# Inverses from 16x16 blocks made row by row on VectorE, and half of the mixers' low parts on GpSimd

## The chip, the cores and the metric
The kernel runs on one core of one Trainium2 chip. The metric is the device time of one execution in microseconds (us); the profile adds, for one such execution, every instruction of the five engines with its start and duration: TensorE (PE, with its weight loads shown apart as PEld), VectorE (DVE), ScalarE (ACT), GpSimd (POOL) and SyncE (SP), which issues the DMAs.

## The reference
A decoder trunk of two layers over 256 tokens of width 2048, all in float32. Each layer is a token mixer followed by a SwiGLU block, both between an adaptive scale and shift (from a conditioning vector `c`) and a layer norm. Layer 0 mixes with mLSTM heads and RWKV-7 heads, layer 1 with retention heads and gated DeltaNet (gdn) heads. Cut to what the change touches:

```python
def _gated_deltanet(q, k, v, z, a, b, conv_w, a_log, dt_bias, norm_g):
    ...
    ut = jnp.eye(CHUNK, dtype=f32) + jnp.where(strict, jnp.einsum('cbhtd,cbhsd->cbhts', kb, kc) * gamma, 0.0)
    u = lax.linalg.triangular_solve(ut, vc * bc[..., None], left_side=True, lower=True)
    ...

def _rwkv7(z, mu, w0, w2, a0, a2, g2, k_k, k_a, r_k, ln_g, ln_b):
    ...
    def step(S, inp):
        rt, wt, kt, vt, at, bt = inp
        sa = jnp.einsum('bhij,bhj->bhi', S, at)
        S = S * wt[:, :, None, :] + sa[..., None] * bt[:, :, None, :] + vt[..., None] * kt[:, :, None, :]
        return S, jnp.einsum('bhij,bhj->bhi', S, rt)
    ...

def _mixer_cd(h, positions, w_in, w_out, ret_norm_g, conv_w, a_log, dt_bias, gdn_norm_g):
    proj = h @ w_in
    ...
    return jnp.concatenate([yc, yd], -1) @ w_out
```
Both recurrences are turned into chunked matrix form (chunks of 128 tokens in the kernel), and each chunk and head needs the inverse of a 128x128 unit triangular matrix. The large products (`h @ w_in` and the like) are dense.

## The kernel before
**Products.** A product of the 256 tokens with 512 columns of weights runs over "units". A unit (`unit`, lines 342 to 359) loads 1 MB of weights into a buffer `raw` (three buffers, shared with the conditioning work), and `split` (lines 326 to 340) turns it into two halves, each as a high part `hi`, rounded by ScalarE (L337), and a low part `lo = raw - hi`, by VectorE (L338). `hi` and `lo` have three buffers each, of one half. For each half, two token tiles and two row blocks, PE does three matmuls: activations high by weights high (L357), high by low (L358), low by high (L359), so 12 matmuls per half and 24 per unit.

**Conditioning.** `ada_unit` (L289) multiplies a 1 MB row block of `ada_w` with `silu(c)` on VectorE and sums it, 192 times in the kernel. `fill` places them behind units at a rate: 48 behind the 44 units of the first mixer, 48 behind the 68 units of the second.

**Inverses.** `rwkv_heads` runs four times (batches of four heads by two chunks) and `gdn_group` twice; each makes eight 128x128 matrices on PE (scores: L776, L1106), writes them to `mk[:, 0]` or `ma[:, 0]`, masks them on GpSimd (`keep_upper` L642, `unit_diagonal` L646) and calls `inverses`. That one starts from inverses of 2x2 blocks (transposes L611, masks L612 on VectorE and L613 on GpSimd) and doubles the block six times, from 2 to 64. A level is: a matmul of the matrix with the blocks so far (L622), a mask (L626, VectorE), a matmul with the transposed blocks (L629), an addition (L632, VectorE), eight transposes (L636) and their copy to `dt` by ScalarE (L637). The results go on to L798 (rwkv) and L1136 (gdn).

**GpSimd** besides: decays of mLSTM (L952, masked at L642) and gdn (L1099), and the sums of the rotary embedding (L1212, L1213).

**Order.** A planner fixes the order on each engine at build time by priorities: program order, with `split` moved ahead by 2000 instructions (`high_priority(offset=2000)`). At run time each engine works through its list in order and waits on semaphores.

**Order of the program:** `first_products` (16 units, before the mixers), `mixer_ab` (rwkv, then mLSTM), `mix_out`, a SwiGLU block, `mixer_cd` (gdn group 0, gdn group 1, retention), `mix_out`, the second SwiGLU block.

Of the kernel before, what the change touches and what calls it, by code (L numbers as in the profile page):

```python
# [13 lines left out]
AF = mybir.ActivationFunctionType  # L14
ALU = mybir.AluOpType
# [4 lines left out]
P = 128  # L20
# [9 lines left out]
LN_EPS = 1e-5  # L30
DH = 128
DECAY = -math.exp(-0.5)
LEVELS = (2, 4, 8, 16, 32, 64)


COLS = {}
# [7 lines left out]

CONS = {}
_n = 0
for _name, _w in [("ident", 128), ("cum", 256), ("tr", 128), ("ones", 128), ("sl", 128), ("m2", 128), ("m2t", 128),
                  ("lev", 64 * len(LEVELS)), ("bones", 128), ("hsel", 2), ("freq", 64)]:
    CONS[_name] = (_n, _w)
    _n += _w  # L50
# [3 lines left out]
def constants():  # L54
    i = np.arange(P)
    c = np.zeros((P, NCONS), np.float32)

    def put(name, a):
        o, w = CONS[name]
        c[:, o:o + w] = a  # L60

    u, t = i[:, None], i[None, :]
    put("ident", np.eye(P))
    after = ((u > 63) & (u <= t)).astype(np.float64) - ((u <= 63) & (u > t))
    before = ((u > 63) & (u < t)).astype(np.float64) - ((u <= 63) & (u >= t))
# [4 lines left out]
    put("m2", (u // 2 == t // 2) & (t <= u))  # L70
    put("m2t", (u // 2 == t // 2) & (u <= t))
# [114 lines left out]
class Trunk:  # L186
    def __init__(self, tc, ins, out, stack):
        self.tc, self.nc, self.ins, self.out = tc, tc.nc, ins, out

        def pool(name, bufs, **kw):  # L190
            return stack.enter_context(tc.tile_pool(name=name, bufs=bufs, **kw))

        self.fix = pool("fix", 1)
        self.raw_p = pool("raw", 3)
        self.split_p = pool("split", 3)
        self.h_p = pool("hp", 4)
        self.a_p = pool("ap", 5)
        self.y_p = pool("yp", 3)
        self.mix = pool("mix", 1)
        self.ps_g = pool("psg", 4, space=PSUM)  # L200
        self.ps_m = pool("psm", 3, space=PSUM)
        self.ps_c = pool("psc", 1, space=PSUM)
        self.dram = pool("scratch", 1, space=DRAM)
        self.n = 0


    def name(self, s):
# [119 lines left out]
    def split(self, src, n, ahead=2000):  # L327

        nc = self.nc
        with self.tc.high_priority(offset=ahead):  # L330
            w = self.raw(src)
            parts = []
            for i in range(2):
                hi = self.split_p.tile([P, 1024], F32R, tag="hi", name=self.name("hi"))
                lo = self.split_p.tile([P, 1024], F32R, tag="lo", name=self.name("lo"))
                ws = w[:, 2 * n * i:2 * n * (i + 1)]
                nc.scalar.activation(hi[:, :2 * n], ws, AF.Copy)  # L337
                nc.vector.tensor_tensor(lo[:, :2 * n], ws, hi[:, :2 * n], ALU.subtract)  # L338
                parts.append((hi, lo))
        return parts  # L340

# [258 lines left out]
    def inverses(self, mt, dd):  # L600


        nc, v = self.nc, self.nc.vector
        d, dt = dd[:, 0], dd[:, 1]
        halves = [slice(0, 4), slice(4, 8)]
        m2, m2t = (self.con(n).unsqueeze(1).to_broadcast([P, 4, P]) for n in ("m2", "m2t"))
        four = lambda x: x.rearrange("p (h t) -> p h t", h=4)
        for hs in halves:
            b = self.bank()
            for j in range(4):  # L610
                nc.tensor.transpose(b[:, P * j:P * j + P], mt[:, hs.start + j, :], self.ident)  # L611
            v.tensor_tensor(d[:, hs, :], four(b[:]), m2, ALU.mult)  # L612
            nc.gpsimd.tensor_tensor(dt[:, hs, :], mt[:, hs, :], m2t, ALU.mult)  # L613
        lev = self.con("lev")
        for n, size in enumerate(LEVELS):
            dv = d.rearrange("p h (n two b) -> p h n two b", two=2, b=size)
            mask = lev[:, 64 * n:64 * n + 64].unsqueeze(1).to_broadcast([P, 4, 64])
            b, p = [], []
            for hs in halves:
                x = self.bank()  # L620
                for j in range(4):
                    nc.tensor.matmul(x[:, 64 * j:64 * j + 64], mt[:, hs.start + j, :], dv[:, hs.start + j, :, 0, :], start=True, stop=True)  # L622
                b.append(x)
            for x in b:
                p.append(self.own([P, 4, 64], "P", 2))
                v.tensor_tensor(p[-1][:], four(x[:, 0:256]), mask, ALU.mult)  # L626
            for hs, x, y in zip(halves, b, p):
                for j in range(4):
                    nc.tensor.matmul(x[:, 256 + 64 * j:320 + 64 * j], dt[:, hs.start + j, :], y[:, j, :], start=True, stop=True)  # L629
            for hs, x in zip(halves, b):  # L630
                o = dv[:, hs, :, 0, :]
                v.tensor_tensor(o, x[:, 256:512].rearrange("p (h n b) -> p h n b", h=4, b=size), o, ALU.add)  # L632
            for hs in halves:
                x = self.bank()
                for j in range(4):
                    nc.tensor.transpose(x[:, P * j:P * j + P], d[:, hs.start + j, :], self.ident)  # L636
                nc.scalar.activation(dt[:, hs, :], four(x[:]), AF.Copy)  # L637
# [7 lines left out]
    def unit_diagonal(self, x, n):  # L645
        self.nc.gpsimd.affine_select(x, x, pattern=[[0, n], [1, P]], compare_op=ALU.not_equal, fill=1.0, base=0, channel_multiplier=-1)  # L646


    def shifted(self, out, src, mu, rows=P):
# [113 lines left out]
    def rwkv_heads(self, B):  # L763
        nc, v = self.nc, self.nc.vector
        mm = nc.tensor.matmul
        ar, bk, rho = B["ar"], B["bk"], B["rho"]
        mk = self.a8([P, 2, 8, P])
        rbkr = self.a8([P, 8, 2, P])
        heads = [(c, h) for c in range(2) for h in range(2)]
        for t in range(NT):  # L770
            for c, h in heads:
                r = slice(64 * h, 64 * h + 64)
                j = 4 * t + 2 * c + h
                b = self.bank()
                for x in range(2):
                    mm(b[:, T * x:T * x + T], bk[r, c, x, t, :], ar[r, c, t].rearrange("p x s -> p (x s)"), start=True, stop=True)  # L776
                nc.scalar.activation(mk[:, 0, j, :], b[:, 0:P], AF.Copy, scale=rho[:, t, 2 * c + h:2 * c + h + 1])
                nc.scalar.activation(mk[:, 1, j, :], b[:, 2 * P:3 * P], AF.Copy)
                v.tensor_copy(rbkr[:, j], b[:].rearrange("p (k x s) -> p k x s", k=2, x=2)[:, :, 1, :])
            js = slice(4 * t, 4 * t + 4)  # L780
            self.keep_upper(mk[:, :, js, :], [2, 4], True)
            self.unit_diagonal(mk[:, 0, js, :], 4)
            self.keep_upper(rbkr[:, js], [4, 2], False)
        dt = self.inverses(mk[:, 0], self.y8([P, 2, 8, P]))
        V = B["vb"][:, 0]
# [2 lines left out]
        for t in range(NT):  # L788
            xb = self.bank()
            for c, h in heads:  # L790
                d = 2 * c + h
# [3 lines left out]
            x = self.t1([P, T])  # L795
# [5 lines left out]
            for c, h in heads:  # L801
                d = 2 * c + h
# [31 lines left out]
        b = self.bank()  # L834
# [216 lines left out]
    def gdn_group(self, g, product, rest, gates=None):  # L1051
# [43 lines left out]
        for t in range(NT):  # L1095
# [166 lines left out]

    def mixer_ab(self, h, rate, early):
        self.yT = {}
        self.rwkv(h, rate, early)
        self.mlstm_gates()
        for g in range(2):
            self.mlstm_group(g, self.ins["w_ab"], h, rate)

    def mixer_cd(self, h, rate):  # L1270
        self.yT = {}
        w = self.ins["w_cd"]
        at = [0]

# [23 lines left out]
            self.retention_group(g, product)  # L1298

    def mix_out(self, w, x, sub):  # L1300
        y = [self.y8([P, D]) for _ in range(NT)]
        self.gate = self.gate_rows()
        stats = [self.tiny([P, 24], "st", 2) for _ in range(NT)]
# [46 lines left out]
```

## Time and profile before

| what | us |
|---|---|
| median of three runs | 2915.05 (2909.9 to 2915.27) |
| the profiled execution | 2917.53 |
| its span, first to last instruction | 2914.8 |
| four rwkv inverses and what lies between them | about 222 to 550 |
| dense products of mLSTM | about 600 to 690 |
| first and second gdn inverse | 1690 to 1740, 1820 to 1890 |
| retention | about 1890 to 2060 |

The page of a profile gives busy time per engine, then groups of equal instructions: line, engine, operation, the tile written and the tiles read, shape, count; then busy time, mean duration in ns, and the idle time of the engine just before them with what ended it. A timeline row is: start, duration, engine, line, operation, tiles, shape, count. A row of the windows is: the stretch, its length, then the busy time of each engine in it. PE's granted clock was 0.976 of full speed over the span. The matmuls' own durations overlap: a 512-column matmul shows 0.39 us and one starts every 0.23 us.

### The profile page before, as it was taken

The page shows a single profiled execution, that of the slowest core. Times are in us where ns is not written, and L with a number is a line of the kernel's source. Part 1 is how long each engine was busy: PE and PEld are TensorE (multiplying, and loading weights), DVE is VectorE, ACT ScalarE, POOL GpSimd, SP SyncE. Part 2 cuts the span into 40 slices and gives each one's busy share as a digit, 9 for nine tenths or more (in the row PEclk, how much of TensorE's full clock was granted, in tenths as well). Part 3 has the DMA queues.
Part 4 walks back from the last instruction along what each step waited for, and adds up shares of the span by engine and source line. Part 5 has one row for each costly group of instructions (what it writes and reads, how often), then busy time and mean ns, then how long its engine had stood idle before and what let it go on. Part 6 is the DMA issues. An engine that isn't in the chain of part 4 may idle for free.

```text
span 2914.8 us, 34843 instructions
## 1 busy us (share of the span) xinstructions
PE 2760.8 (95%) x13466; PEld 2291.6 (79%) x13466; DVE 2011.9 (69%) x2955; ACT 1276.3 (44%) x1685; POOL 123.5 (4%) x114
## 2 busy tenths in 40 slices
PE   3699999999999999999998999999989999999997
PEld 2578887877778888888887888877878888888886
DVE  7876666687777557767758878687786545556556
ACT  2264345446454444444445545343444444443442
POOL 0001111020000000000000121101000000000000
PEclk9799999999999999999999999999999999999998
DMA  9974234367578668867855756477656656667563
GB/s 366 356 277 170 91 134 159 131 242 267 199 249 305 249 219 296 297 236 275 305 197 205 295 209 241 159 277 295 216 202 231 249 195 224 242 220 241 192 216 130
DMA packets 106189, 674.62 MB, mean 231 GB/s; under 512 B 12068, under 2 KB 14248, under 8 KB 28328
## 3 DMA queue, kind: packets, MB, share of 16 engines
q1 hardware_dynamic: 106024, 672.41, 64.1%
q8 instruction: 105, 1.72, 0.2%
q14 instruction: 60, 0.49, 0.0%
HBM read 663.97 MB, written 8.39 MB: 231 GB/s over the span
## 4 chain that ended last, share of the span: by engine, by line
PE 62%; DVE 5%; DMA 3%; issue 1%; ACT 1%; POOL 1%; POOLq 0%; DVEq 0%; ACTq 0%
PE g L359 19%; PE g L358 19%; PE g L357 19%; DMA raw<-ada 2%; DVE lo L338 2%; DVE raw L289 1%; PE m L622 1%; PE m L629 1%; PE m L575 1%; ACT hi L337 1%; DMA raw<-gu 1%; DMA raw<-w_cd 0%; PE m L524 0%; PE c L317 0%; PE m L636 0%
## 5 line engine op out<-in xcount | busy, mean ns | idle before, releaser
L338 DVE TENSOR_TENSOR lo<-raw,hi 128x1024 fp32r<-128x1024 f32 (+2 forms) x848 | 1025.4, 1215 | 653.6 <-ACT hi L337 650.3
L337 ACT ACTIVATE hi<-raw 128x1024 fp32r<-128x1024 f32 (+2 forms) x848 | 885.7, 1049 | 1165.6 <-PE g L359 1004.1
L357 PE MATMUL g<-hi,h 128*128 128x512 f32 (+3 forms) x2368 | 932.7, 396 | 80.3 <-ACT hi L337 76.5
L358 PE MATMUL g<-lo,h 128*128 128x512 f32 (+3 forms) x2368 | 934.1, 395 | 3.8 <-DVE lo L338 3.8
L359 PE MATMUL g<-hi,h 128*128 128x512 f32 (+3 forms) x2368 | 930.9, 394 | 0.0
L357 PEld LDWEIGHTS g<-hi,h 128*128 128x128 f32 x2368 | 451.9, 191 | 172.0 <-ACT hi L337 78.8
L358 PEld LDWEIGHTS g<-lo,h 128*128 128x128 f32 x2368 | 452.6, 191 | 95.2 <-DVE lo L338 9.1
L359 PEld LDWEIGHTS g<-hi,h 128*128 128x128 f32 x2368 | 452.0, 191 | 88.6 <-issue 2.7
L289 DVE SCALAR_TENSOR_TENSOR raw<-raw,silu_c 128x2048 f32<-128x2048 f32 x176 | 404.4, 2298 | 23.1 <-DMA raw<-ada 22.8
L359 PE MATMUL g<-hi,a 128*128 128x512 f32 x960 | 374.5, 390 | 0.0
L357 PE MATMUL g<-hi,a 128*128 128x512 f32 x960 | 374.4, 390 | 0.0
L358 PE MATMUL g<-lo,a 128*128 128x512 f32 x960 | 374.1, 390 | 0.1
L358 PEld LDWEIGHTS g<-lo,a 128*128 128x128 f32 x960 | 180.3, 188 | 37.4 <-DVE lo L338 0.5
L359 PEld LDWEIGHTS g<-hi,a 128*128 128x128 f32 x960 | 180.3, 188 | 36.9
L357 PEld LDWEIGHTS g<-hi,a 128*128 128x128 f32 x960 | 180.2, 188 | 37.0
L1099 POOL TENSOR_SCALAR s<-cons_sb,log_alpha 128x128 f32<-128x128 f32 x16 | 22.9, 1446 | 1040.6 <-PE g L359 903.4
L637 ACT ACTIVATE y<-m 128x512 f32<-128x512 f32 x48 | 27.4, 595 | 78.3 <-PE m L636 78.1
L902 DVE SCALAR_TENSOR_TENSOR f<-c,cols_sb,f 128x255 f32<-128x255 f32 (+2 forms) x120 | 57.2, 477 | 6.2 <-ACT f L900 5.1
L626 DVE TENSOR_TENSOR P<-m,cons_sb 128x256 f32<-128x256 f32 x72 | 30.1, 423 | 43.6 <-PE m L622 43.2
L629 PEld LDWEIGHTS m<-P,y 128*128 128x128 f32 x384 | 50.0, 203 | 2.1 <-issue 0.3
L622 PEld LDWEIGHTS m<-y,a 128*128 128x128 f32 x384 | 49.7, 205 | 0.8
L622 PE MATMUL m<-y,a 128*128 128x64 f32 x384 | 49.7, 283 | 0.0
(376 smaller groups left out, 2051.2 us busy)
## 6 DMA issues: line engine op xcount, KB each, us to landing
raw<-ada SPq DMA_DIRECT2D x176, 1024.0 KB, 5.5
raw<-gu SPq DMA_DIRECT2D x176, 1024.0 KB, 4.8
raw<-dn SPq DMA_DIRECT2D x88, 1024.0 KB, 4.8
raw<-w_cd SPq DMA_DIRECT2D x60, 1024.0 KB, 5.0
raw<-w_ab SPq DMA_DIRECT2D x56, 1024.0 KB, 5.5
a<-ada SPq DMA_DIRECT2D x16, 1024.0 KB, 11.3
raw<-o_ab SPq DMA_DIRECT2D x16, 1024.0 KB, 5.0
raw<-o_cd SPq DMA_DIRECT2D x16, 1024.0 KB, 4.9
```

Of the source, the lines that this page charges most:

```text
L289: v.scalar_tensor_tensor(w[:], w[:], 1.0, self.sc[:], ALU.mult, ALU.mult, accum_out=m[:, i:i + 1])
L337: nc.scalar.activation(hi[:, :2 * n], ws, AF.Copy)
L338: nc.vector.tensor_tensor(lo[:, :2 * n], ws, hi[:, :2 * n], ALU.subtract)
L357: mm(o, ah, wh, start=first, stop=False)
L358: mm(o, ah, wl, start=False, stop=False)
L359: mm(o, al, wh, start=False, stop=stop and k == 3)
L575: nc.tensor.transpose(b[:, P * k:P * k + P], gs[:, t, P * k:P * k + P], self.ident)
L622: nc.tensor.matmul(x[:, 64 * j:64 * j + 64], mt[:, hs.start + j, :], dv[:, hs.start + j, :, 0, :], start=True, stop=True)
L626: v.tensor_tensor(p[-1][:], four(x[:, 0:256]), mask, ALU.mult)
L629: nc.tensor.matmul(x[:, 256 + 64 * j:320 + 64 * j], dt[:, hs.start + j, :], y[:, j, :], start=True, stop=True)
L637: nc.scalar.activation(dt[:, hs, :], four(x[:]), AF.Copy)
L902: v.scalar_tensor_tensor(o[:, d:T], z[:, 0:T - d], self.col(wname, c + 3 - d), o[:, d:T], ALU.mult, ALU.add)
```

## The change
Two parts. In `inverses` the start from 2x2 blocks and the first three levels (2, 4, 8) give way to inverses of the 16x16 diagonal blocks, made on VectorE alone. The strictly upper part of each block is cut out of `mt` (four masks, one for each 32 partitions, since a block lies on the diagonal) and held as 16 columns (`u`); `e` starts as `u` plus the unit diagonal, and for k from 14 down to 1 row k of each block is spread to its 16 partitions (`stream_shuffle`), multiplied with column k of `u`, and added to the columns behind k. `dt` is then `e` set on the diagonal; `d` is its transpose, by PE and ScalarE. Three levels follow (16, 32, 64). The row loop has priority 4000. The masks on GpSimd of the matrix to be inverted go away (`unit_diagonal`, and the half of `keep_upper` that worked on it).

In `split` the low part of the second half is made by GpSimd while `shared` is set, which is during `mixer_ab` and `mixer_cd`: 44 and 68 units.

```diff
-LEVELS = (2, 4, 8, 16, 32, 64)
+BASE = 16
+LEVELS = (16, 32, 64)
...
+    c32, c16 = np.arange(32)[None], np.arange(BASE)[None]
+    put("tri", (u % 32 // BASE == c32 // BASE) & (u % BASE < c32 % BASE))
+    put("diag", u % BASE == c16)
+    put("blk", u // BASE == np.arange(P // BASE)[None])
...
-                nc.vector.tensor_tensor(lo[:, :2 * n], ws, hi[:, :2 * n], ALU.subtract)
+                e = nc.gpsimd if self.shared and i else nc.vector
+                e.tensor_tensor(lo[:, :2 * n], ws, hi[:, :2 * n], ALU.subtract)
...
+        with self.tc.high_priority(offset=4000):
+            e2 = self.t1([P, 8, 2, BASE])
+            for q in range(4):
+                r = slice(32 * q, 32 * q + 32)
+                o = CONS["tri"][0]
+                v.tensor_tensor(e2[r], mt[r, :, r].rearrange("p h (a c) -> p h a c", a=2),
+                                self.cons[r, o:o + 32].rearrange("p (a c) -> p a c", a=2).unsqueeze(1).to_broadcast([32, 8, 2, BASE]), ALU.mult)
+            u, e, f = (self.own([P, 8, BASE], "e1", 3) for _ in range(3))
+            v.tensor_tensor(u[:], e2[:, :, 0, :], e2[:, :, 1, :], ALU.add)
+            v.tensor_tensor(e[:], u[:], self.con("diag").unsqueeze(1).to_broadcast([P, 8, BASE]), ALU.add)
+            for k in range(BASE - 2, 0, -1):
+                n = BASE - 1 - k
+                x = f[:, :, k + 1:]
+                v.stream_shuffle(x, e[:, :, k + 1:], [k] * 16 + [16 + k] * 16)
+                v.tensor_tensor(x, x, u[:, :, k:k + 1].to_broadcast([P, 8, n]), ALU.mult)
+                v.tensor_tensor(e[:, :, k + 1:], e[:, :, k + 1:], x, ALU.add)
         for hs in halves:
+            v.tensor_tensor(dt[:, hs, :].rearrange("p h (n c) -> p h n c", c=BASE), e[:, hs, :].unsqueeze(2).to_broadcast([P, 4, 8, BASE]),
+                            self.con("blk").unsqueeze(1).unsqueeze(3).to_broadcast([P, 4, 8, BASE]), ALU.mult)
             b = self.bank()
             for j in range(4):
-                nc.tensor.transpose(b[:, P * j:P * j + P], mt[:, hs.start + j, :], self.ident)
-            v.tensor_tensor(d[:, hs, :], four(b[:]), m2, ALU.mult)
-            nc.gpsimd.tensor_tensor(dt[:, hs, :], mt[:, hs, :], m2t, ALU.mult)
+                nc.tensor.transpose(b[:, P * j:P * j + P], dt[:, hs.start + j, :], self.ident)
+            nc.scalar.activation(d[:, hs, :], four(b[:]), AF.Copy)
...
-            self.keep_upper(mk[:, :, js, :], [2, 4], True)
-            self.unit_diagonal(mk[:, 0, js, :], 4)
+            self.keep_upper(mk[:, 1, js, :], [4], True)
...
-            self.keep_upper(ma[:, 0, js, :], [4], True)
-            self.unit_diagonal(ma[:, 0, js, :], 4)
...
     def mixer_ab(self, h, rate, early):
         self.yT = {}
+        self.shared = True
...
     def mixer_cd(self, h, rate):
         self.yT = {}
+        self.shared = True
...
     def mix_out(self, w, x, sub):
+        self.shared = False
```

More of the change, by code (lines that the diff above doesn't have):

```diff
@@ L46 @@
 _n = 0
-for _name, _w in [("ident", 128), ("cum", 256), ("tr", 128), ("ones", 128), ("sl", 128), ("m2", 128), ("m2t", 128),
+for _name, _w in [("ident", 128), ("cum", 256), ("tr", 128), ("ones", 128), ("sl", 128), ("tri", 32), ("diag", 16), ("blk", 8),
                   ("lev", 64 * len(LEVELS)), ("bones", 128), ("hsel", 2), ("freq", 64)]:
@@ L69, in constants @@
     put("sl", u > t)
-    put("m2", (u // 2 == t // 2) & (t <= u))
-    put("m2t", (u // 2 == t // 2) & (u <= t))
+    c32, c16 = np.arange(32)[None], np.arange(BASE)[None]
+    put("tri", (u % 32 // BASE == c32 // BASE) & (u % BASE < c32 % BASE))
+    put("diag", u % BASE == c16)
+    put("blk", u // BASE == np.arange(P // BASE)[None])
     lev = []
@@ L605, in inverses @@
         halves = [slice(0, 4), slice(4, 8)]
-        m2, m2t = (self.con(n).unsqueeze(1).to_broadcast([P, 4, P]) for n in ("m2", "m2t"))
         four = lambda x: x.rearrange("p (h t) -> p h t", h=4)
+        with self.tc.high_priority(offset=4000):
[14 more added lines that the diff above has]
+                v.tensor_tensor(e[:, :, k + 1:], e[:, :, k + 1:], x, ALU.add)
         for hs in halves:
+            v.tensor_tensor(dt[:, hs, :].rearrange("p h (n c) -> p h n c", c=BASE), e[:, hs, :].unsqueeze(2).to_broadcast([P, 4, 8, BASE]),
+                            self.con("blk").unsqueeze(1).unsqueeze(3).to_broadcast([P, 4, 8, BASE]), ALU.mult)
             b = self.bank()
             for j in range(4):
-                nc.tensor.transpose(b[:, P * j:P * j + P], mt[:, hs.start + j, :], self.ident)
-            v.tensor_tensor(d[:, hs, :], four(b[:]), m2, ALU.mult)
-            nc.gpsimd.tensor_tensor(dt[:, hs, :], mt[:, hs, :], m2t, ALU.mult)
+                nc.tensor.transpose(b[:, P * j:P * j + P], dt[:, hs.start + j, :], self.ident)
+            nc.scalar.activation(d[:, hs, :], four(b[:]), AF.Copy)
         lev = self.con("lev")
@@ L643, in keep_upper @@
                                      fill=0.0, base=0, channel_multiplier=-1)
-    def unit_diagonal(self, x, n):
-        self.nc.gpsimd.affine_select(x, x, pattern=[[0, n], [1, P]], compare_op=ALU.not_equal, fill=1.0, base=0, channel_multiplier=-1)
     def shifted(self, out, src, mu, rows=P):
@@ L1300, in mix_out @@
     def mix_out(self, w, x, sub):
+        self.shared = False
         y = [self.y8([P, D]) for _ in range(NT)]
```

## The prediction

> **What bounds the kernel now.** I read the page first, then the windows of the two mixers, the chain of waits, and the timeline of one inverse.
>
> ```profile
> PE 2760.8 (95%) x13466; PEld 2291.6 (79%) x13466; DVE 2011.9 (69%) x2955; ACT 1276.3 (44%) x1685; POOL 123.5 (4%) x114
> ...
> L338 DVE TENSOR_TENSOR lo<-raw,hi 128x1024 fp32r<-128x1024 f32 (+2 forms) x848 | 1025.4, 1215 | 653.6 <-ACT hi L337 650.3
> L337 ACT ACTIVATE hi<-raw 128x1024 fp32r<-128x1024 f32 (+2 forms) x848 | 885.7, 1049 | 1165.6 <-PE g L359 1004.1
> ```
> TensorE is the bound over the whole: ScalarE stands idle because it waits for TensorE (L359) to give back buffers. GpSimd is nearly unused. The change touches the two mixers; in the windows below the columns are length, then busy time of PE, PEld, DVE, ACT and POOL. The first two rows are the four rwkv inverses and the first gdn inverse. The third, a sum line, adds three stretches in which products lie densely (600 to 690, 1570 to 1690, 1890 to 2060).
>
> ```profile
> 222.00:550.00 328.00, 313.98 (x2010) 269.14 (x2010) 205.68 (x464) 147.05 (x286) 43.71 (x37) 0.96 0.37 129
> 1690.00:1740.00 50.00, 49.93 (x355) 45.47 (x353) 38.55 (x63) 19.09 (x30) 8.75 (x7) 1.00 0.57 195
> ...
> sum 380.00, PE 366.35 PEld 301.64 DVE 313.40 ACT 188.38 POOL 40.42; mean PE 122.12 PEld 100.55 DVE 104.47 ACT 62.79 POOL 13.47
> ```
> PE is busy 96% in both, but VectorE differs: 63% (206 of 328) in the rwkv stretch, 82% (313 of 380) in the dense ones. So work taken from PE is worth most around the inverses, and work that loads VectorE or its neighbour hurts most in the dense stretches.
>
> **The change part by part.**
>
> *PE loses three of six levels per inverse.* From the critical chain, inside one gdn inverse:
>
> ```profile
> 1706.31 1.73 PE m L629 x16
> 1709.70 0.87 PE m L636 x8
> 1710.58 1.73 PE m L622 x16
> ```
> A level costs PE 1.73 + 0.87 + 1.73 = 4.33 us. Six inverses (four rwkv, two gdn) times three levels is 18 levels, 77.9 us: 52.0 in rwkv, 26.0 in gdn. The transposes of L611 stay, eight per inverse, now fed from `dt`.
>
> *VectorE gets the 16x16 blocks.* Rows for its prices by size (16, 256 and 512 elements per partition), and the pace of dependent small operations:
>
> ```profile
> L430 DVE TENSOR_TENSOR v<-v,v 128x16 f32<-128x16 f32 x14 | 2.4, 172 | 0.3
> L750 DVE TENSOR_TENSOR y<-f,f 128x256 f32<-128x256 f32 x8 | 3.3, 417 | 0.0
> L1087 DVE TENSOR_TENSOR q<-m,v 128x512 f32<-128x512 f32 x4 | 2.7, 687 | 0.0
> L626 DVE TENSOR_TENSOR P<-m,cons_sb 128x256 f32<-128x256 f32 x72 | 30.1, 423 | 43.6 <-PE m L622 43.2
> L289 DVE DVE_READ_ACCUMULATOR raw<-raw,silu_c 128x1 f32 x176 | 14.4, 82 | 0.0
> ...
> 585.93 0.18 DVE L430 TENSOR_TENSOR v<-v,v 128x16 f32<-128x16 f32 x1
> 586.14 0.18 DVE L431 TENSOR_SCALAR v<-v 128x16 f32<-128x16 f32 x1
> ```
> From 16 to 256 elements the price rises by 245 ns, about 1.0 ns each; a dependent successor starts 0.21 us after its predecessor, 0.04 more than the price. Per inverse: four masks of 256 elements, 4 x 0.42 = 1.7; `u` and `e`, 128 elements each, 2 x 0.28 = 0.6; 14 rounds of a shuffle and two tensor_tensors on 8 to 112 elements (mean 60), 42 x (0.172 + 44 x 0.001 + 0.04) = 42 x 0.256 = 10.7; two block masks of 512 elements, 1.4. Together 14.4 us. The trace has no shuffle. I price it as the other small operations; its bounds are the 0.172 row below and, if it issues a second instruction, 0.08 more (the accumulator read), 14 x 0.08 = 1.1 us. [...] Gone are two L612 (as L1087, 1.4) and twelve operations of the size of L626 (5.1). VectorE is busier by about 8 us per inverse, 48 in all.
>
> *What this does to the inverse's length.* The second rwkv inverse, from its last scores to its last copy (the last line is L338 alone in the windows of 222 to 550):
>
> ```profile
> 313.94 1.99 PE L776 MATMUL m<-y 64*128 64x256 f32 x12 [0.22 <-DVE a L779]
> ...
> 322.80 1.59 PE L622 MATMUL m<-y,a 128*128 128x64 f32 x7
> ...
> 364.04 0.60 ACT L637 ACTIVATE y<-m 128x512 f32<-128x512 f32 x1 [0.27 <-PE m L636]
> ...
> sum 328.00, DVE 43.69; mean DVE 43.69
> ```
> Scores end at 315.9; 6.9 us go to GpSimd's masks and the transposes, then six levels take 41.8 us, 7.0 each; 48.7 in all. Afterwards the GpSimd masks of this operand are gone and the row chain takes their place: 14.4 + about 1.5 for transposes and copies + 3 x 7.0 = 36.9 us if nothing slips between its 42 steps. But the gaps between dependent steps are open to other ready VectorE work. Without the inverses' own share (4 x 6.5 for L612 and three levels that go, 4 x 5 for the levels that stay) and half of the low parts (22 us), VectorE is busy 206 - 46 - 22 = 138 of 328 us, 42%; at that share 14.4 us stretch to 25 and the inverse takes 47.5. So the length falls by between 1 and 12 us.
>
> In rwkv the saving lies between the length alone at its worst (4 x 1 = 4) and PE's whole 52: PE was 96% busy there, which speaks for the upper end, but four batches follow one another through the inverse and only some products are at hand to fill. I take 30. In gdn, PE's 49.93 of 50 and products at hand speak for the whole 26, VectorE's load (38.6 of 50, plus 8, plus GpSimd's new work) against it; ends 0 and 26, I take 18.
>
> *GpSimd makes 112 low parts.* `shared` is set for 44 units in the first mixer and 68 in the second, eight of them half as wide.
>
> ```profile
> L613 POOL TENSOR_TENSOR y<-a,cons_sb 128x512 f32<-128x512 f32 x8 | 10.3, 1282 | 0.3
> L1212 POOL TENSOR_TENSOR zt<-zt,f 128x256 f32<-128x256 f32 x8 | 5.9, 738 | 157.4 <-DVE f L1209 116.4 <-ACT a L381 41.0
> ...
> 1679.20 0.39 PE L357 MATMUL g<-hi,h 128*128 128x512 f32 x1
> 1679.43 0.40 PE L358 MATMUL g<-lo,h 128*128 128x512 f32 x1
> ```
> 256 more elements cost 0.544 us, so 1024 cost 1.282 + 2 x 0.544 = 2.37 us, where VectorE takes 1.22. VectorE gives up 104 x 1.22 + 8 x 0.69 = 132 us; GpSimd gains 104 x 2.37 + 8 x 1.28 = 257 us. Time at hand: a half unit is 12 matmuls at 0.227 us, 2.73 us; `hi` has three buffers, so ScalarE writes a half two halves (5.45 us) ahead of its use and, after its own 1.05, leaves 4.4 us for the low part. 2.37 fits. But:
>
> ```profile
> 1856.01 0.73 POOL L1212 TENSOR_TENSOR zt<-zt,f 128x256 f32<-128x256 f32 x1 [25.89 <-DVE f L1209]
> 1985.06 2.77 POOL L1213 TENSOR_TENSOR zt<-zt,f 128x256 f32<-128x256 f32 x1
> ...
> 1856.18 0.41 DVE L1211 TENSOR_TENSOR f<-g,cos 128x256 f32<-128x256 f32 x1
> ...
> 1984.86 2.39 DVE L289 SCALAR_TENSOR_TENSOR raw<-raw,silu_c 128x2048 f32<-128x2048 f32 x1
> ...
> 1987.18 2.80 DVE L289 SCALAR_TENSOR_TENSOR raw<-raw,silu_c 128x2048 f32<-128x2048 f32 x1
> ```
> The same 256-element operation on GpSimd takes 0.73 beside a VectorE operation whose first input lies in PSUM, and 2.77 beside L289, which reads two SBUF tensors: it ends 0.6 us after the first L289, and the second L289 is stretched from 2.3 to 2.80. So GpSimd and such operations take turns. Behind one L289 a low part needs 2.3 + 2.37 = 4.7 of 4.4 us; behind an L289 and an L338, 5.9. VectorE's own two-input operations, the row chain's among them, wait up to 2.37 in turn, and everything queued behind them waits with them. In the dense stretches there are about 55 second halves (the row below: 137 us of L338 is 111 halves). Ends: less than nothing, -4 (VectorE's relief, first halves come sooner), and 55 x 1.5 = 82 us; the row nearest is L289's share there (102.5 of 380, 27%, with 0.3 us late each, some 4 us), so I take 8.
>
> Queued behind low parts on GpSimd are L1099, L952, the score masks and L1212/L1213, some 20 groups; PE waits for them through L1100, L997 and L1219. Each can come one low part later: ends 0 and 20 x 2.37 = 47, I take 8, since PE has products between.
>
> *At nothing:* ScalarE's copies fall from twelve to eight per inverse, two of them new (0.6 each, hidden by an engine that is 44% busy; on the path the two would cost 7 us in six inverses); the constants shrink; no DMA is added. The raw buffer of a unit comes free some 1.2 us later, hidden while the DMA is ahead; that is in the 82.
>
> **Sum.** -30 - 18 + 8 + 8 = -32 us on the profiled execution (2917.5 us, of which the span is 2914.8). The median of the runs is 2.5 us lower, 2915.05, so 2883.
>
> **The rivals.**
>
> *R1, PE's whole time comes out.* The row chain is filled with products and the low parts stay within 4.4 us: -78, and 4 for late low parts: 2841 us. For it: PE at 96 to 100% around every inverse. Against it: the batches' order in rwkv.
>
> *R2, GpSimd and VectorE block one another, slower.* Place: the dense stretches.
>
> ```profile
> sum 380.00, DVE 136.63; mean DVE 45.54
> ...
> sum 380.00, DVE 102.53; mean DVE 34.18
> ```
> (L338 and L289 alone, in the same three stretches.) VectorE would hold 313 - 68 = 245 us, GpSimd 68 x 2.37/1.22 + 40 = 172: together 417 in 380, 37 too many if they never overlap. Only VectorE's other work, 245 - 103 - 68 = 74 us, can lie beside GpSimd. If none of it does, these stretches grow by 37, gdn gains nothing, rwkv only some 18: +19, 2934 us. It decides once less than about 20 of those 74 us overlap. [...]
>
> *R3, the row chain eats its gain.* Other work and locks stretch every chain to 25 us or more: rwkv 4, gdn 9, low parts and queues +16: +3, 2918 us. For it: dependent small chains are interleaved in this trace; against it: PE had work.
>
> **How the numbers follow.** A measurement of this kernel can tell some 0.2% (6 us) from no change. Forecast 0.46, R1 0.20, R2 0.21, R3 0.13. Faster: forecast 0.44, R1 0.20, R3 0.03 = 0.67. Same: R3 0.07, and 0.02 each from forecast and R2 = 0.11. Slower: R2 0.19, R3 0.03 = 0.22. The range runs from R1 to R2, 2842 to 2932; half of each of them lies outside, about 0.2.
>
> **What would show it.** Right: 18 fewer levels, PE's busy time down by 70 us or more; L338's GpSimd rows near 2.4 to 3.5 us; a row chain of 15 to 25 us; the time from last scores to last L637-type copy under 45 us; the second gdn inverse likewise. Wrong: GpSimd's low parts with a mean over 4 us, PE idle at the matmul that reads `lo`, L289 and L338 well above 2.3 and 1.2 us (R2); chains over 25 us with PE idle before the first level (R3). The sum is wrong if shuffles cost much more than 0.25 us, or if the planned order puts the chain so late that PE waits for it in turn.

## The result and the profile after

| what | before | after |
|---|---|---|
| median of the runs, us | 2915.2 (2909.9 to 2918.5) | 2961.1 (2955.7 to 2965.3) |
| ratio | | 1.0158, interval 1.0134 to 1.0182 |
| profiled span, us | 2914.8 | 2961.9 |

The change makes the kernel 46 us slower. The forecast was 2883, in a range of 2842 to 2932; the result lies outside it, on the side of R2 and beyond R2's own 2934.

The page of the changed kernel, its busy line and the groups that answer to those of before:

```profile
PE 2720.0 (92%) x12746; PEld 2235.3 (75%) x12746; DVE 2055.8 (69%) x3143; ACT 1269.6 (43%) x1665; POOL 374.0 (13%) x198
...
L341 ACT ACTIVATE hi<-raw 128x1024 fp32r<-128x1024 f32 (+2 forms) x848 | 886.7, 1049 | 1244.0 <-PE g L364 1001.8
L343 DVE TENSOR_TENSOR lo<-raw,hi 128x1024 fp32r<-128x1024 f32 (+1 forms) x736 | 911.3, 1241 | 659.0 <-ACT hi L341 656.0
...
L343 POOL TENSOR_TENSOR lo<-raw,hi 128x1024 fp32r<-128x1024 f32 (+2 forms) x112 | 297.0, 2652 | 1614.3 <-DVE v L495 835.6
L293 DVE SCALAR_TENSOR_TENSOR raw<-raw,silu_c 128x2048 f32<-128x2048 f32 x176 | 423.7, 2407 | 77.6 <-DMA raw<-ada 77.2
```
PE has 13466 - 12746 = 720 matmuls fewer, the 18 levels of 40, so that part was done as announced. The odd number is VectorE's: it gave 112 low parts away, some 130 us of work, and is busy 44 us longer than before (2011.9). The means hardly say why: 1241 ns for a low part instead of 1215, 2407 for the conditioning operation (L289 before, L293 now) instead of 2298 (L289's mean on the page of before).

Next, windows of both kernels cut where the first transposes of each layer norm (L529 here, L524 before) start on PE. Columns: stretch, length, busy PE, PEld, DVE, ACT, POOL, then PE's granted clock, DMA share, GB/s. Of before, the first mixer's stage and the second's:

```profile
0.00:801.40 801.40, 701.76 (x3789) 582.42 (x3789) 574.54 (x1060) 355.97 (x573) 64.77 (x66) 0.95 0.59 217
...
1552.30:2155.70 603.40, 578.25 (x3038) 486.25 (x3038) 479.71 (x842) 278.61 (x410) 58.75 (x48) 0.98 0.66 237
```
and of after:

```profile
0.00:806.70 806.70, 668.40 (x3309) 541.14 (x3310) 616.62 (x1216) 353.25 (x561) 162.41 (x94) 0.92 0.58 216
...
1558.10:2202.20 644.10, 570.68 (x2799) 471.70 (x2799) 481.53 (x875) 274.96 (x402) 209.26 (x103) 0.95 0.61 222
```
The first mixer's stage is 5.3 us longer and the second's 40.7; the two SwiGLU stages stay within 1 us. In both stages PE has less to do, and the time goes up all the same.

Where the time sits is seen in the timeline of the changed kernel (start, duration, engine, line). VectorE's side of three places:

```profile
261.15 2.38 DVE L627 TENSOR_TENSOR e<-e,e 128x80 f32<-128x80 f32 x1
263.56 0.24 DVE L628 TENSOR_TENSOR e<-e,e 128x80 f32<-128x80 f32 x1
...
283.37 4.45 DVE L293 SCALAR_TENSOR_TENSOR raw<-raw,silu_c 128x2048 f32<-128x2048 f32 x1
...
1616.58 2.37 DVE L435 TENSOR_TENSOR v<-v,v 128x16 f32<-128x16 f32 x1
1618.98 0.17 DVE L436 TENSOR_SCALAR v<-v 128x16 f32<-128x16 f32 x1
```
and GpSimd's at the same places:

```profile
261.05 2.38 POOL L343 TENSOR_TENSOR lo<-raw,hi 128x1024 fp32r<-128x1024 f32 x1 [2.70 <-ACT hi L341]
...
283.32 2.36 POOL L343 TENSOR_TENSOR lo<-raw,hi 128x1024 fp32r<-128x1024 f32 x1 [9.80 <-ACT hi L341]
...
1616.48 2.43 POOL L343 TENSOR_TENSOR lo<-raw,hi 128x1024 fp32r<-128x1024 f32 x1 [4.81 <-ACT hi L341]
```
In these rows a VectorE operation that starts 0.05 to 0.1 us behind a low part of GpSimd gets its work done only when that one has ended: 0.25 us of work on 80 elements takes 2.38 and ends 0.10 us behind it, a 16-element operation takes 2.37 instead of 0.17 and ends 0.04 us behind it, and the conditioning operation takes 4.45 instead of 2.28 and ends 2.14 us behind it, nearly its whole own length. Set every VectorE operation against the median of its shape in the kernel with the rows alone (first experiment): in the changed kernel 94 operations are more than 0.1 us late, by 138.5 us together, against 6.4 us in 16 operations before. Some 29 us of it fall on two lines of the row chain (L627, L628), 21 on the conditioning operation and 20 on VectorE's own low parts. That is how 130 us of relief vanish, and the group means hide it.

PE's waits, after (engine, line, what it waited for, us, times, longest):

```profile
PE g L363 <- DVE lo L343: 24.4, 20, 4.7
...
PE c L1235 <- POOL zt L1229: 11.2, 5, 3.9
PE c L710 <- DVE e L628: 10.1, 2, 5.1
PE m L634 <- DVE y L630: 7.8, 3, 3.6
PE m L931 <- DVE q L1183: 7.6, 2, 4.5
PE c L913 <- DVE e L628: 7.2, 1, 7.2
...
PE g L363 <- POOL lo L343: 1.6, 1, 1.6
```
and before:

```profile
PE g L358 <- DVE lo L338: 3.8, 9, 0.5
```
In the change PE waits for VectorE all over the mixers: low parts, row chain (L628, L630), convolutions (L913), heads (L931). The 24.4 us are waits for low parts that VectorE makes; for those of GpSimd PE waits 1.6 us. What comes late is VectorE's work, not the work that was moved.

### The profile page after: what moved, and what is told of

It reads as the page before. It is cut to its first block, busy times and chain, and to the rows that moved or that the text cites. A ratio compares the mean times of both kernels' runs of the same rounds, so it can differ in the third digit from the quotient of the medians.

```text
span 2961.9 us, 33724 instructions
## 1 busy us (share of the span) xinstructions
PE 2720.0 (92%) x12746; PEld 2235.3 (75%) x12746; DVE 2055.8 (69%) x3143; ACT 1269.6 (43%) x1665; POOL 374.0 (13%) x198
## 5 line engine op out<-in xcount | busy, mean ns | idle before, releaser
L343 DVE TENSOR_TENSOR lo<-raw,hi 128x1024 fp32r<-128x1024 f32 (+1 forms) x736 | 911.3, 1241 | 659.0 <-ACT hi L341 656.0
L362 PEld LDWEIGHTS g<-hi,h 128*128 128x128 f32 x2368 | 458.2, 194 | 177.8 <-ACT hi L341 81.2
L364 PEld LDWEIGHTS g<-hi,h 128*128 128x128 f32 x2368 | 457.6, 193 | 90.7 <-issue 2.2
L343 POOL TENSOR_TENSOR lo<-raw,hi 128x1024 fp32r<-128x1024 f32 (+2 forms) x112 | 297.0, 2652 | 1614.3 <-DVE v L495 835.6
L293 DVE SCALAR_TENSOR_TENSOR raw<-raw,silu_c 128x2048 f32<-128x2048 f32 x176 | 423.7, 2407 | 77.6 <-DMA raw<-ada 77.2
L532 ACT ACTIVATE t<-m,affine 128x128 f32<-128x128 f32 x96 | 35.0, 473 | 31.4 <-PE m L529 26.4
L405 ACT ACTIVATE t<-t,affine 128x256 f32<-128x256 f32 x16 | 8.7, 590 | 76.4 <-DVE affine L302 76.3
L627 DVE TENSOR_TENSOR e<-e,e 128x8 f32<-128x8 f32 (+6 forms) x84 | 36.2, 431 | 2.0
L293 DVE SCALAR_TENSOR_TENSOR a<-a,silu_c 128x2048 f32<-128x2048 f32 x16 | 36.6, 2286 | 0.4 <-DMA a<-ada 0.4
L529 PE MATMUL m<-cons_sb,y 128*128 128x128 f32 x96 | 16.5, 314 | 19.7 <-DVE v L497 18.6
```

Of the source, the lines that this page charges most:

```text
L293: v.scalar_tensor_tensor(w[:], w[:], 1.0, self.sc[:], ALU.mult, ALU.mult, accum_out=m[:, i:i + 1])
L343: e.tensor_tensor(lo[:, :2 * n], ws, hi[:, :2 * n], ALU.subtract)
L362: mm(o, ah, wh, start=first, stop=False)
L364: mm(o, al, wh, start=False, stop=stop and k == 3)
L405: nc.scalar.activation(h32[:, j, :], x[:, j, :], AF.Identity, bias=self.ab[:, 16 + k:17 + k], scale=self.ab[:, k:k + 1])
L529: nc.tensor.transpose(b[:, P * j:P * j + P], y[t][:, P * k:P * k + P], self.ident)
```

## The experiments

Theories at the start: T1, GpSimd's low parts and VectorE's operations on two SBUF tensors block one another; T2, the serial row chain is itself the loss; T3, only both together cost. Each ratio is to the kernel before.

**1. The two halves of the change, apart.** The rows alone are the change with `e = nc.vector` in `split`; the low parts alone are before with the two lines of `split` and the four of `shared`.

```diff
-                e = nc.gpsimd if self.shared and i else nc.vector
+                e = nc.vector
```


> The changed kernel with every low part on VectorE again; only the row-made inverses stay. If GpSimd's low parts and VectorE's two-input operations block one another and that is the loss (T1), this is faster than before: 2865 to 2900 us, as TensorE has 78 us less to do and the row chain takes 15 to 25 us per inverse. If the serial row chain itself is the loss (T2), it is slower than before: 2930 to 2965 us, and the row chains still take 30 to 43 us as in the changed kernel.

> The kernel before with only GpSimd's 112 low parts added; the inverses stay as they were. T1: slower than before by more than the change as a whole, 2960 to 3000 us, with VectorE's 2048-element conditioning operation (2.30 us before) near 2.4 and GpSimd's low part near 2.7 us. T2: no difference worth naming, 2905 to 2925 us. If only the two parts together lose (T3), this and the rows alone are each no slower than before.

Rows alone: 2864.9 us, 0.9837 (0.9812 to 0.9862). Low parts alone: 3028.5 us, 1.0396 (1.0374 to 1.0419). T1 had given 2865 to 2900 and 2960 to 3000: the first time lies at the lower end of its range, the second above its range, so the direction came and the sizes were too small. The rows bring 50 us, and the low parts cost 113 without them and 2961 - 2865 = 96 with them. T2 falls as the cause of the loss, T3 too. The rows' gain by stages is 23.2 and 28.6 us:

```profile
0.00:778.20 778.20, 656.94 (x3308) 531.79 (x3308) 598.56 (x1260) 349.67 (x560) 39.47 (x50) 0.93 0.60 224
...
1528.00:2102.80 574.80, 552.09 (x2799) 459.52 (x2799) 486.81 (x942) 272.75 (x402) 41.04 (x36) 0.98 0.68 248
```

**2. The row chain's priority, and the place of the low parts.** The first kernel is the rows alone without the `high_priority(offset=4000)` around the chain; the second is the change with `shared` left off in `mixer_cd`.

```diff
-        with self.tc.high_priority(offset=4000):
+        with self.tc.high_priority(offset=0):
...
     def mixer_cd(self, h, rate):
-        self.shared = True
```


> As the rows alone, but the row loop without its priority of 4000. If the priority matters because it pushes the low parts of the products aside, this is faster than the rows alone by 10 us or more; if the priority is what keeps the chain short, it is slower by 10 us or more; under T1 neither: within 10 us of the rows alone.

> The changed kernel with GpSimd's low parts in the first mixer only (44 units), VectorE's in the second. The two profiles put 41 of the 46 us of loss between the second and the third norm, that is in the second mixer. T1: that loss goes and the two gdn inverses gain: 2890 to 2925 us. T2: the gdn chains stay long and most of the loss stays, 2940 to 2960 us.

Without the priority 2872.1 us, 0.9868 (0.9837 to 0.9900): 7 us more than with it, and the two intervals overlap; whether the priority is worth anything stays open. With low parts in the first mixer alone 2894.7, 0.9935 (0.9910 to 0.9959): the 44 units of the first mixer cost 30 us of the 96, the 68 of the second 66: 0.7 and 1.0 us a unit. The loss isn't confined to one place.

**3. What of a low part on GpSimd costs.** Three candidates: M1, the lock between the engines; M2, the low part comes too late at the products (2.65 us instead of 1.23, buffers held longer); M3, another order of the work. Two kernels on the base of the rows alone, VectorE making all low parts. In the first, GpSimd does the same amount of two-input work beside each of the 112 second halves, for nobody. In the second, VectorE's low part is only delayed, by work of GpSimd that reads one column.

```diff
+                if self.shared and i:
+                    nc.gpsimd.tensor_tensor(w[:, :2 * n], self.sc[:, :2 * n], hi[:, :2 * n], ALU.subtract)
```


> The row-by-row inverse as in the change, every low part on VectorE (2864.9 us in the run above). New: at each of the 112 places where the change gives a low part to GpSimd, GpSimd subtracts two other SBUF tensors of the same size and writes into the half of the raw tile that is already spent. No low part waits for it; only the raw tile comes free later. M1, two-input work of GpSimd and of VectorE in SBUF hold one another up: at least 60 of the 96 us that lie between the change (2961) and this kernel without the extra work come back, so 2925 to 2965, with VectorE's conditioning operation at 2400 ns or above in the mean and worst ones above 4000. M2, the low part itself comes too late at the products: at most 20 us, 2865 to 2885. M3, another order of the work by the planner: no clear forecast, near 2865.

```diff
+                if self.shared and i:
+                    nc.gpsimd.tensor_copy(lo[:, 0:1], hi[:, 0:1])
+                    for _ in range(2):
+                        nc.gpsimd.memset(lo[:, :2 * n].bitcast(F32), 0.0)
                 nc.vector.tensor_tensor(lo[:, :2 * n], ws, hi[:, :2 * n], ALU.subtract)
```


> The row-by-row inverse, every low part on VectorE, but ahead of each of the 112 second halves GpSimd copies one column of the high part to the low tile and then fills the low tile twice with zeros, about 2 us in all by the memsets of before (0.313 us at 256 elements, 0.111 at 8). VectorE's subtraction waits for that, so the low part comes some 2 us later than alone, and VectorE, in order, stands still at some of them; GpSimd reads one column only and never two SBUF tensors. M2 (lateness): 50 us or more of the 96 come back, 2915 or above. M1 (contention): at most 30 us, 2865 to 2895, and VectorE's conditioning operation stays near 2300 ns.

The idle subtraction: 3045.0 us, 1.0456 (1.0422 to 1.0491), 180 us over the rows alone; M1 had given 60 to 100, so M1's direction came and its size was too small. The delay: 2905.5 us, 0.9973 (0.9956 to 0.9990), 41 us over, between what the two theories gave. The delay also makes VectorE itself stand and wait for GpSimd's fills (64.6 us in 48 waits), which the change does not do. The page of the kernel with the idle subtraction:

```profile
PE 2744.0 (90%) x12746; PEld 2243.0 (74%) x12746; DVE 2226.6 (73%) x3255; ACT 1266.7 (42%) x1664; POOL 425.3 (14%) x198
...
L345 POOL TENSOR_TENSOR raw<-silu_c,hi 128x1024 f32<-128x1024 f32 (+2 forms) x112 | 340.3, 3038 | 1555.7 <-DVE v L497 813.1
...
L293 DVE SCALAR_TENSOR_TENSOR raw<-raw,silu_c 128x2048 f32<-128x2048 f32 x176 | 440.9, 2506 | 33.5 <-DMA raw<-ada 33.4
```
VectorE has the same 3255 operations as in the rows alone and is busy 2226.6 - 2042.2 = 184 us longer. The span is 177 us longer.

**4. The lock taken out of both.** In the idle work (first kernel) and in the change itself (second kernel; its edit is shown), GpSimd's subtraction gives way to a copy of one column and three fills with zeros that together last as long; nothing but the column is read. In the second kernel the low part of the second half is therefore left out (zeros), with VectorE relieved and the products waiting as in the change. A third leaves these low parts out without any work of GpSimd, with the high part multiplied in their place: the most that the relief can bring.

```diff
-                e.tensor_tensor(lo[:, :2 * n], ws, hi[:, :2 * n], ALU.subtract)
+                if self.shared and i:
+                    nc.gpsimd.tensor_copy(lo[:, 0:1], hi[:, 0:1])
+                    for m in (2 * n, 2 * n, n):
+                        nc.gpsimd.memset(lo[:, :m].bitcast(F32), 0.0)
+                else:
+                    nc.vector.tensor_tensor(lo[:, :2 * n], ws, hi[:, :2 * n], ALU.subtract)
```


> As the kernel before it in which GpSimd subtracts two other SBUF tensors beside each of the 112 second halves (3045.0 us), but GpSimd copies one column and then only fills the same dead half of the raw tile with zeros, about 2.9 us at each place (0.47 + 0.96 + 0.96 + 0.53 by the rows of the run with fills ahead of the low part). The raw tile is held as long as there, but GpSimd reads one column only. Lock (two-input GpSimd work and VectorE hold one another up): most of the 180 us go, 2865 to 2895. Held raw tiles or GpSimd's mere occupation: 2980 or above.

> The change itself, but in the second halves GpSimd copies one column of the high part and fills the low tile with zeros (about 2.9 us, against 2.75 us for its subtraction in the change), so the low part is left out there, VectorE is relieved of the same work, the products wait for the low tile as long as in the change, and GpSimd no longer reads two SBUF tensors. Lock: the 96 us that the change lost against the rows alone go, 2885 or below. Lateness of the low part at the products: 2930 or above. Both in equal parts: about 2910.

> The row-by-row inverse alone, and the low parts of the 112 second halves are left out: the high part is multiplied in their place, TensorE's work is the same. VectorE loses 112 x 1.2 = 134 us of work, the most that any other engine could take from it here. If VectorE's load in the mixers sets part of the time: 2865 falls by 30 us or more, to 2835 or below. If it does not: 2855 to 2866, and there was nothing to win by moving low parts.

Fills beside: 2922.9 us, 1.0030 (1.0011 to 1.0050). Of the 180 us, 122 go with the two-input reading; 58 stay, more than the lock theory gave (0 to 30); the held raw tiles, GpSimd's occupation and the order of the work can each have a part in them and were not told apart. Fills in place: 2848.5 us, 0.9773 (0.9758 to 0.9788), so 112.6 us of the change go with the subtraction's reading. Left out: 2815.0 us, 0.9655 (0.9637 to 0.9674), 50 us under the rows alone: taking these low parts off VectorE is worth something. The page of the change with fills:

```profile
PE 2684.7 (94%) x12746; PEld 2213.2 (78%) x12746; DVE 1936.5 (68%) x3143; ACT 1271.7 (45%) x1666; POOL 399.8 (14%) x534
...
L293 DVE SCALAR_TENSOR_TENSOR raw<-raw,silu_c 128x2048 f32<-128x2048 f32 x176 | 402.9, 2289 | 37.3 <-DMA raw<-ada 37.2
...
L343 POOL CAST lo<-hi 128x1 fp32r<-128x1 f32 x112 | 65.0, 580 | 1460.7 <-ACT hi L341 1460.7
L345 POOL MEMSET lo<- 128x1024 f32 (+2 forms) x336 | 265.0, 789 | 18.8
```
GpSimd is busier than in the change (399.8 against 374.0), and the low tile is ready 3.3 us after its high part on average, against 2.8 in the change: later, not sooner. VectorE, with the same 3143 operations, is busy 119 us less, the excess of the late operations falls from 138.5 to 24.3 us, and the conditioning operation is back at 2289 ns. So lateness is not what the change lost by, and the lock is.

Besides the reading, the raw tile differs between the change and the fills in place. In the change it is held until GpSimd has read it, with the fills only until ScalarE has; ScalarE's waits for the weights of the second mixer (`raw<-w_cd`) are 67.6 us in the change and 15.8 with the fills. The 113 us therefore contain what the held tile costs. In the pair beside, the raw tile is held in both kernels and the products are the same, and the reading is still worth 122 us. The kernel with the low parts left out gets its raw tiles back sooner as well (22.5 us of such waits, 50.7 in the rows alone), so its 50 us are not VectorE's load alone.

Standing still is also not the whole of the loss. The page of the fills beside begins:

```profile
PE 2709.9 (93%) x12746; PEld 2223.1 (76%) x12746; DVE 2051.2 (70%) x3255; ACT 1263.8 (43%) x1665; POOL 451.4 (15%) x534
```
The same 12746 matmuls keep PE busy 2720.0 us in the change and 2684.7 with the fills in place, at a mean granted clock of 0.961 and 0.973: 35 of the 113 us. The other 78 are PE idle. In the pair beside it is 34 us of busy time (clock 0.955 and 0.964) and 90 us of idle time. The clock is lower in the kernel in which PE idles more; whether it follows from that was not tested.

The windows of the change with the fills in place, and those of the kernel with these low parts left out:

```profile
0.00:741.50 741.50, 642.37 (x3309) 523.71 (x3309) 555.50 (x1216) 352.54 (x561) 165.71 (x226) 0.95 0.63 235
...
1494.40:2089.20 594.80, 559.67 (x2799) 464.87 (x2800) 425.09 (x875) 276.67 (x403) 231.48 (x304) 0.96 0.66 240
```

```profile
0.00:732.80 732.80, 638.84 (x3309) 521.35 (x3309) 550.02 (x1216) 347.21 (x557) 38.28 (x50) 0.96 0.64 237
...
1483.80:2056.30 572.50, 550.21 (x2798) 458.79 (x2799) 417.32 (x875) 276.29 (x403) 36.75 (x36) 0.98 0.68 249
```
The lengths of these windows, from kernel to kernel, give the account of the change in the profiled executions (us):

| step | first mixer | second mixer |
|---|---|---|
| rows alone against before | -23.2 | -28.6 |
| 112 low parts left out, raw tiles free sooner (left out against rows) | -45.4 | -2.3 |
| GpSimd's work without the reading (fills in place against left out) | +8.7 | +22.3 |
| lock, with the raw tiles held (change against fills in place) | +65.2 | +49.3 |
| sum | +5.3 | +40.7 |

One thing stays open. The planner lays each kernel's work out anew: of the 3146 VectorE instructions that the trace has for the change, and as many for the kernel with fills in place, 2415 stand in the same order. How much of a step is order (M3) was not separated. That the lock came out as 113 and as 122 us on two bases, and that VectorE's excess falls by 114 us with it, speaks against a large share.

**5. The length of the row chain, and a faster kernel.** The rows alone with other blocks: 8x8 (6 steps, four levels), 32x32 (30 steps, two levels), and 8x8 in the first mixer with 16x16 in the second.

```diff
-BASE = 16
-LEVELS = (16, 32, 64)
+BASE = 8
+LEVELS = (8, 16, 32, 64)
```


> The row-by-row inverse alone, from 8x8 blocks: six row steps in place of 14 and one level of products more for each inverse, 6 x 4.33 = 26 us more on TensorE than with 16x16 blocks and about half the chain on VectorE. If TensorE's work sets the time and the chain on VectorE costs nothing: 2885 to 2895 (+20 to +30 on 2864.9). If the chain costs something by itself: under 2875.

> The row-by-row inverse alone, from 32x32 blocks: 30 row steps in place of 14 and one level of products fewer, 26 us less on TensorE and, with steps of up to twice the width, some 17 us more on VectorE for each inverse. If TensorE's work sets the time and the chain costs nothing: 2838 to 2850. If the longer chain reaches the end of the products that cover it: 2865 or above.

> The row-by-row inverse alone, from 8x8 blocks in the first mixer (its stage ended 9.2 us earlier with them) and 16x16 in the second (there 8x8 cost 9.9 us): 2850 to 2858 if the two stages add up as they did in those runs.

8x8: 2863.8 us, 0.9826 (0.9799 to 0.9852), as fast as 16x16 though PE makes a level more in each inverse. 32x32: 3011.6 us, 1.0340 (1.0307 to 1.0374). Mixed: 2854.6 us, 0.9797 (0.9778 to 0.9816). The stage of the first mixer lasts 769.0 us with 8x8 against 778.2, although PE has 4 x 4.33 = 17 us more to do there; by that sum, an estimate, the longer chain costs about 27 us in it. In the second, 8x8 makes the stage 584.7 instead of 574.8, 10 us for 9 us of PE work: there the chain was covered. So the statement that the chain costs nothing, which experiment 1 seemed to allow, is wrong for the first mixer. PE's waits with 32x32 show the chain uncovered:

```profile
PE m L632 <- DVE y L628: 79.6, 4, 25.9
...
PE m L632 <- DVE a L628: 20.5, 2, 19.5
```
L632 is the first transpose behind the chain: 100 us in six waits. The mixed kernel takes the better half of each, 768.9 and 572.3 us, and beats both the kernel before and the change: 61 us under before, 2.0% by the ratio.

## Why the prediction was wrong, step by step

- **PE loses 18 levels: right.** 720 matmuls, and the time they bring: -30 and -18 forecast, -23.2 and -28.6 measured with the rows alone. The sum of 48 against 52 fits, and PE's busy time falls by 71.0 us there, as announced (70 or more); in the change it falls by 40.8 only, at a lower granted clock (0.961, against 0.976 before and 0.97 with the rows alone), for which the sum had no term. The split did not fit: the first mixer has a chain cost that the second covers.
- **The row chain, 14.4 us alone: its prices were right, its length not.** A shuffle takes 230 ns on average (a step was taken at 0.256, with 0.04 of gap in it), the mask load that comes with each 13 ns (0.08 were the bound). The forecast stretched the chain to 25 us; in the changed kernel the first inverse's chain runs from the first L618 to the last L630, 231.9 to 275.2:

```profile
L618 DVE TENSOR_TENSOR s<-a,cons_sb x4: 405/420/758, 231.9 to 233.6; 32x256 f32<-32x256 f32 x4
```

```profile
L630 DVE TENSOR_TENSOR y<-e,cons_sb x2: 679/686/692, 270.6 to 274.5; 128x512 f32<-128x512 f32 x2
```
  That is 43.3 us, and the six take 20 to 43 (20.9 to 54.6 with the rows alone). From the last scores to the last copy the four rwkv inverses take 39 to 69 us (45 to 51 before): the length did not fall by 1 to 12 us. R3 was right about the chain's length and wrong about its price: it left a gain of 13 us, and the rows alone gain 50.
- **GpSimd's low part, 2.37 us alone: right.** The shortest take 2.35, the median 2.40, the mean of the full width 2.75.
- **The 8 us for late low parts, between -4 and 82: the failed step.** With the 8 us for the queue behind them, the sum had +16 for GpSimd's low parts; they cost 96 (2961 - 2865). The step asked when a low part arrives, took the conditioning operation's share of the time with 0.3 us for each as the price, came to some 4 us and doubled it without a reason. Two terms lay in it unseparated: leaving the low parts out is worth 50 us (-4 was the lowest bound), and the lock, with the raw tiles held, costs 113 (82 was the highest), about 1.0 us for each of the 112 low parts. What GpSimd's work costs without the reading, 34 us (2849 - 2815), would have been within the bounds.
- **R2 named the mechanism and gave it the wrong place and measure.** It added the busy time of two engines in the dense stretches (417 in 380 us) and charged only what would not fit: +37 there. But the lock is paid also where both engines have time to spare. In the change, 71 of VectorE's tensor_tensor and scalar_tensor_tensor operations with all inputs in SBUF started beside a low part of GpSimd and more than 0.2 us ahead of its end; 69 of them were over 0.1 us late, by 1.8 us in the median. The lock, with the raw tiles held, comes to 65 us in the first mixer's stage, in which VectorE is busy 77% of the time (598.56 of 778.20 us with the rows alone) and where small operations of the row chain (L627) take up to 2.4 us. The sentence that VectorE's two-input operations "wait up to 2.37 in turn, and everything queued behind them waits with them" stood in the prediction and had no term in the sum; at the 1.0 us for each low part that the runs show, such a term would have turned the sum's sign. The lock works the other way round as well: in the change the low part at 1946.99 us started 0.04 us behind a conditioning operation, took 4.52 us, against 2.40 in the median, and ended 2.26 us after that operation's end.
- **R1, 2841:** with the lock taken out the change takes 2848.5. That it lies near is luck: R1 had -78 for PE's levels and +4 for late low parts, and the runs have -50 for the rows, -50 for the low parts left out and +34 for GpSimd's work without the reading.
- **The signs.** "A mean over 4 us" for the low part and conditioning "well above 2.3" were set as signs of R2; 2.65 and 2.41 came, and R2's mechanism was there. A wait that strikes 94 operations out of 3143 shows in maxima and in the timeline, not in means. PE idle at the matmul that reads `lo` was a sign that did come, 24.4 us against 3.8 (7.4 with the rows alone), but at the low parts of VectorE; at those of GpSimd it is 1.6.
- **The POOL queue, +8:** PE waits 11.2 us for L1229 (6.2 us for its counterpart before). The term was not isolated.

## What to carry to other kernels

Before work moves from VectorE to GpSimd, ask how many VectorE operations read two SBUF tensors while GpSimd does too (69 of 71 were late here; beside fills it was two of 226, as the last section shows), and charge each meeting with the rest of the other's operation, not with a share of busy time. Small operations in a serial chain can pay the whole length of a large one (2.38 us for 0.25 at L627), so a long GpSimd operation can do most harm beside such a chain. The table's lock row fits that, though the two mixers differ in more: 1.5 us a unit in the first (65.2 for 44), which has four chains, and 0.7 in the second (49.3 for 68), which has two. And an engine's relief and the cost of its helper are two terms: a kernel that leaves the moved work out measures the first, one that replaces it by fills of the same length measures the second without the lock. In both, look at which buffers become free sooner than in the change.

## What was not expected of the hardware

- Some operations with one SBUF tensor are caught as well: of 12 tensor_scalar operations of this kind that started beside a low part in the change and more than 0.2 us ahead of its end, 8 were over 0.1 us late; of five shuffles none was late by more than 0.01. L436 is a tensor_scalar on 16 elements; in the rows alone and in the change (minimum, median, maximum in ns):

```profile
L436 DVE TENSOR_SCALAR v<-v x14: 166/174/177, 613.5 to 1590.1; 128x16 f32<-128x16 f32 x14
```

```profile
L436 DVE TENSOR_SCALAR v<-v x14: 163/174/2373, 621.3 to 1626.8; 128x16 f32<-128x16 f32 x14
```
- Fills catch these too, but not the operations with two. The tensor_scalar and the tensor_tensor line before it in the change with fills in place, where a fill takes 0.95 us:

```profile
L440 DVE TENSOR_SCALAR v<-v x14: 163/220/946, 559.5 to 1564.8; 128x16 f32<-128x16 f32 x14
```

```profile
L439 DVE TENSOR_TENSOR v<-v,v x14: 162/174/177, 559.3 to 1562.5; 128x16 f32<-128x16 f32 x14
```
  Of 226 VectorE operations with two inputs in SBUF that started beside a fill and no other GpSimd operation, two were late, and both started while VectorE had a tensor_scalar held up. The longest conditioning operation takes 3.18 us there, as with the rows alone, and 4.46 in the change.
- GpSimd's copy of a single column takes 0.188 us in the median and up to 2.35 in the change with fills in place; the row does not show what stood beside it:

```profile
L343 POOL CAST lo<-hi x112: 181/188/2346, 161.0 to 1977.3; 128x1 fp32r<-128x1 f32 x112
```
- VectorE operations with one input in PSUM and one in SBUF were not stretched: in the change 92 of them ran beside a low part of GpSimd, and none was over 0.04 us above the median of its shape. L654 is one of the lines:

```profile
L654 DVE TENSOR_TENSOR y<-m,y x24: 414/424/425, 279.0 to 592.2; 128x256 f32<-128x256 f32 x24
```
